# Sums of x's blocks on GpSimd instead of VectorE, and double units three and eight instead of four and seven, in a hybrid decoder trunk

## The chip, the cores and the metric

The kernel runs on one core of one Trainium2 chip: TensorE (PE), VectorE (DVE), ScalarE (ACT), GpSimd (POOL) and SyncE (SP), which work from their own queues, each strictly in the order of its program, and wait for each other on semaphores. The metric is the device time of one execution in microseconds (us).

## The reference

Two layers, each `LN(alpha*x + 0.5*SwiGLU(x))`, `LN(alpha*x + mixer(x))`, `LN(alpha*x + 0.5*SwiGLU(x))`, for 256 positions of width 1024, all in float32. The change touches the SwiGLUs (FFNs), of which there are four:

```python
def swiglu(x, w_in, w_out):
    gate, up = jnp.split(x @ w_in, 2, axis=-1)
    return (jax.nn.silu(gate) * up) @ w_out
```

with `w_in` 1024 x 5632 and `w_out` 2816 x 1024. The mixer (three attention branches, gates, projections) stands between the first and the second FFN of a layer.

## The kernel before

**Tiles.** The 256 positions are two halves, t=0 and t=1, of 128. A float32 product is made of three passes: x and each weight are split into a high and a low part (hi, lo), and TensorE adds x_hi*w_hi, x_hi*w_lo and x_lo*w_hi in one PSUM bank (L585, L586, L587; in double units L784, L786, L787). XH and XL hold the parts of the transposed x of each half, in eight blocks of 128.

**Weights.** A chunk is 128 x 1024 elements, loaded by SyncE into one of seven raw buffers (L306). ScalarE writes its high part (L340) and VectorE, with two SBUF inputs, its low part (L348) into r buffers, of which there are 28. A chunk feeds six matmuls of 512 columns for each half (a turn).

**Units of an FFN.** The 2816 inner columns are eleven units of 256, numbered 0 to 10. `in_unit(u)` makes a unit's gate and up columns (four chunks), `h_chain` its SiLU and product (ScalarE L628, VectorE L630) and its transposed split (ScalarE L488, VectorE L490, which reads a PSUM bank and one SBUF tile). `out_unit` (o0 to o10, two chunks each) multiplies by `w_out`. A **double unit** D covers two units u and u+1 for both halves at once, by seven products P1 to P7 instead of eight (a scheme like Strassen's): joint chunks that serve t=0 and t=1 together, two to a product, 14 in all. Its weights are sums too: VectorE adds chunks (L328), and GpSimd issues DMAs that add into the wide buffers (L318, behind a VectorE addition). Its x operands a2, s2, s4, s3 are sums of x's blocks over both halves, made once in an FFN by `s_chain`: ten additions of 128 x 512 (L654, called through `tt`), and behind each result a split: ScalarE copies the high part (L663), VectorE subtracts (L665). Its results are combined by VectorE (L718, L720, L729).

**Order.** The order of the units in each FFN is the string `FFN` (L64): a number is an `in_unit`, oN an `out_unit`, DN a double unit. A planner in the kernel keeps a clock for each engine (`clk`, `spend`, `V` and `A` for the costs of a VectorE and a ScalarE instruction) and writes each engine's program from it: t=1 follows t=0 by up to seven chunks, and by two around double units. `s_chain` is a generator that starts when x's last block is ready (`hooks`); each `yield` is the time at which it goes on. At the kernel's start VectorE also makes tables for the mixer from about 52 us on (L361 to L438).

Of the kernel before, what the change touches and what calls it, by code (L numbers as in the profile page):

```python
# [57 lines left out]
SEM = 0.4  # L58
# [2 lines left out]

FFN = "0 1 o0 2 o1 3 o2 D4 o3 6 o4 o5 D7 o6 9 o7 10 o8 o9 o10"  # L64
NEAR = 2

MIXER = "qi sm ga0 ka ga1 qa va gc0 qc gc1 oa0 qb oa1 gb0 oc0 oc1 gb1 ob0 ob1"
# [110 lines left out]
def kernel(ctx: ExitStack, tc: tile.TileContext, x, positions, w_in, sink_b, w_br_a, w_br_b, w_br_c,  # L178
                      w_out, ffn1_in, ffn1_out, ffn2_in, ffn2_out, ln_g, ln_b, out):
    nc = tc.nc  # L180
    pe, dve, act, pool = nc.tensor, nc.vector, nc.scalar, nc.gpsimd
# [7 lines left out]
    clk = {"act": 0.0, "dve": 0.0, "pool": 0.0, "dma": 0.0}  # L189

    def spend(engine, cost):
        clk[engine] = max(clk[engine], vt[0]) + cost
        return clk[engine]

    def V(n):
        return spend("dve", 0.07 + 0.00104 * n)

    def A(n, extra=0.1):
        return spend("act", extra + 0.00084 * n)
# [266 lines left out]
    def mark(key, at):  # L466
        ready[key] = at + SEM
        if key in hooks:
            start(hooks.pop(key)(), 1, at + SEM)
# [151 lines left out]
    def ffn(sub, wi2, wo2):  # L621
# [23 lines left out]
        def block(t, h):  # L645
            return [T[t][:, 4 * h:4 * h + 4, :].rearrange("p k c -> p (k c)").bitcast(F32) for T in (XH, XL)]
# [4 lines left out]
        def s_chain():  # L651

            def tt(out, a, b, op):
                dve.tensor_tensor(out, a, b, op=op)  # L654
                return V(512) + 0.05

            def split(name, f):
                while (r := R.take()) is None:
                    yield vt[0] + LATER
                held[0] -= 1  # L660
                yield clk["dve"] + SEM
                hi, lo = r.t[:, :512], r.t[:, 512:]
                act.activation(hi, f.t, AF.Copy)  # L663
                yield A(512) + SEM
                dve.tensor_tensor(lo, f.t, hi.bitcast(F32), op=OP.subtract)  # L665
                mark(("s", sub, name), V(512))
                S[name] = r

            held[0] += 4
            f = []  # L670
            while len(f) < 3:
                if (b := F.take(3)) is None:
                    yield vt[0] + LATER
                else:
                    f.append(b)
            a, b, c = f
            (h11, l11), (h12, l12), (h21, l21), (h22, l22) = (block(*e) for e in ((0, 0), (0, 1), (1, 0), (1, 1)))
            yield tt(a.t, h21, h22, OP.subtract)
            yield tt(b.t, l21, l22, OP.subtract)
            yield tt(a.t, a.t, b.t, OP.add)  # L680
            yield from split("a2", a)
            yield tt(b.t, a.t, h11, OP.subtract)
            yield tt(b.t, b.t, l11, OP.subtract)
            yield from split("s2", b)
            yield tt(c.t, b.t, h12, OP.add)
            yield tt(c.t, c.t, l12, OP.add)
            yield from split("s4", c)
            yield tt(a.t, h11, h21, OP.subtract)
            yield tt(b.t, l11, l21, OP.subtract)
            yield tt(a.t, a.t, b.t, OP.add)  # L690
            yield from split("s3", a)
            for e in f:
                e.free(clk["dve"])
# [160 lines left out]

        steps = FFN.split()
        doubles = [e for e in steps if e[0] == "D"]
# [639 lines left out]
```

## Time and profile before

| | |
|---|---|
| time, median of 3 runs | 1230.28 us (1229.1 to 1230.42) |
| profiled execution, its own time | 1229.19 us |
| its span, first to last instruction | 1227.4 us |
| ScalarE busy | 697.3 us |
| L348, VectorE, low halves of weights | 526.4 us in 440 instructions |
| L340, ScalarE, high halves | 449.1 us in 440 instructions |
| DMA, mean rate | 188 GB/s |

Busy times are sums over the span; the profile's slices are fortieths of the span (30.7 us), each digit a tenth of it. In lists of instructions the columns are the start in us from the span's start, the duration, engine, line, operation, output<-inputs and, in brackets, the idle time before it and what ended that; "x3" merges three that follow each other. In lists of waits the columns are the waiting engine and what it makes, the engine and result waited for, and then us in total, times, longest.

### The profile page before, as it was taken

The numbers are of one execution on the slowest core, as the hardware profiler recorded it, in microseconds if no ns is written. First come the engines' busy times: TensorE is split into PE (matmuls) and PEld (weight loads), VectorE is DVE, ScalarE is ACT, GpSimd is POOL, SyncE is SP. The second block draws the span as 40 slices with busy tenths as digits, with TensorE's granted clock in tenths as the row PEclk, the third lists the DMA queues.
The fourth block names the chain that finished last, engine by engine and source line by source line (L and its number), as shares of the span: only waits on it lengthen the run. The fifth ranks groups of instructions, "written<-read, shape, count | busy, mean of one in ns | idle before, by whom it ended". The sixth has DMA issues, their size and how long they took to land.

```text
span 1227.4 us, 16445 instructions
## 1 busy us (share of the span) xinstructions
PE 1213.3 (99%) x5801; PEld 1007.1 (82%) x5801; DVE 1028.8 (84%) x1677; ACT 697.3 (57%) x1061; POOL 50.5 (4%) x94
## 2 busy tenths in 40 slices
PE   8999999999999999999999999999999999999997
PEld 6888888888887888888888888888888878888886
DVE  7789969996999977888697888699969999788874
ACT  7464744566676545656454755554666665456640
POOL 0101000000000000010000010000000000000100
PEclk9999999999999999999999999999999999999999
DMA  9849685554535755688565678655535467567650
GB/s 339 244 125 286 218 237 158 152 146 145 172 114 178 224 172 177 194 247 269 179 214 159 217 214 291 157 162 155 155 120 154 121 199 235 166 172 249 197 189 35
DMA packets 160179, 231.32 MB, mean 188 GB/s; under 512 B 18272, under 2 KB 79712, under 8 KB 160096
## 3 DMA queue, kind: packets, MB, share of 16 engines
q1 hardware_dynamic: 153760, 215.59, 55.4%
q0 software_dynamic: 6336, 14.68, 5.6%
q8 instruction: 45, 0.74, 0.2%
q14 instruction: 38, 0.31, 0.1%
HBM read 229.19 MB, written 1.05 MB: 188 GB/s over the span
## 4 chain that ended last, share of the span: by engine, by line
PE 91%; DVE 7%; ACT 1%; issue 1%; DVEq 0%; ACTq 0%
PE bank L586 24%; PE bank L587 23%; PE bank L585 23%; PE bank L476 5%; PE bank L786 4%; PE bank L787 4%; PE bank L784 4%; DVE r L348 2%; PE bank L1024 1%; PE bank L1023 1%; PE bank L1196 1%; PE bank L1129 1%; DVE r L974 0%; DVE iacc L1054 0%; ACT r L340 0%
## 5 line engine op out<-in xcount | busy, mean ns | idle before, releaser
L348 DVE TENSOR_TENSOR r<-raw,r 128x1024 fp32r<-128x1024 f32 (+1 forms) x440 | 526.4, 1217 | 49.8 <-ACT r L340 35.6
L340 ACT ACTIVATE r<-raw 128x1024 fp32r<-128x1024 f32 (+1 forms) x440 | 449.1, 1052 | 78.3 <-PE bank L587 17.6
L585 PE MATMUL bank<-r,xh 128*128 128x512 f32 (+1 forms) x928 | 369.5, 398 | 0.0
L586 PE MATMUL bank<-r,xh 128*128 128x512 f32 (+1 forms) x928 | 361.8, 390 | 1.1 <-DVE r L348 1.1
L587 PE MATMUL bank<-r,xl 128*128 128x512 f32 (+1 forms) x928 | 361.9, 390 | 0.0
L587 PEld LDWEIGHTS bank<-r,xl 128*128 128x128 f32 x928 | 174.2, 188 | 36.7 <-DVE xl L490 0.2
L586 PEld LDWEIGHTS bank<-r,xh 128*128 128x128 f32 x928 | 174.7, 188 | 34.9 <-DVE r L348 2.8
L585 PEld LDWEIGHTS bank<-r,xh 128*128 128x128 f32 x928 | 174.5, 188 | 31.9 <-ACT r L340 0.2
L585 PE MATMUL bank<-r,r 128*128 128x512 f32 x448 | 179.8, 401 | 0.0
L587 PE MATMUL bank<-r,r 128*128 128x512 f32 x448 | 175.1, 391 | 0.0
L586 PE MATMUL bank<-r,r 128*128 128x512 f32 x448 | 174.9, 390 | 0.1
L488 ACT ACTIVATE r<-bank 128x256 fp32r<-128x256 f32 (+1 forms) x104 | 49.7, 482 | 119.5 <-PE bank L476 113.9
L587 PEld LDWEIGHTS bank<-r,r 128*128 128x128 f32 x448 | 84.1, 188 | 18.1
L586 PEld LDWEIGHTS bank<-r,r 128*128 128x128 f32 x448 | 84.3, 188 | 16.3 <-DVE r L348 0.9
L585 PEld LDWEIGHTS bank<-r,r 128*128 128x128 f32 x448 | 84.2, 188 | 15.1
L628 ACT ACTIVATE f<-bank 128x256 f32<-128x256 f32 x54 | 20.7, 382 | 114.2 <-PE bank L587 113.8
L490 DVE TENSOR_TENSOR r<-bank,r 128x256 fp32r<-128x256 f32 (+1 forms) x104 | 55.6, 542 | 29.8 <-ACT r L488 28.8
L476 PE MATMUL bank<-ident,f 128*128 128x128 f32 x388 | 61.6, 273 | 2.3 <-DVE f L1176 2.3
L476 PEld LDWEIGHTS bank<-ident,f 128*128 128x128 f32 x388 | 48.6, 140 | 18.0 <-DVE f L1176 4.3
L786 PE MATMUL bank<-r,r 128*128 128x512 f32 x128 | 49.9, 390 | 0.3 <-DVE r L348 0.3
L488 ACT ACTIVATE xh<-bank 128x512 fp32r<-128x512 f32 x32 | 19.1, 597 | 54.4 <-PE bank L476 50.0
L784 PE MATMUL bank<-r,r 128*128 128x512 f32 x128 | 49.9, 390 | 0.0
(193 smaller groups left out, 1290.3 us busy)
## 6 DMA issues: line engine op xcount, KB each, us to landing
raw<-in_ffn_in_dram SPq DMA_DIRECT2D x224, 256.0 KB, 4.0
raw<-in_w_in_dram SPq DMA_DIRECT2D x96, 512.0 KB, 3.7
raw<-in_ffn_out_dram SPq DMA_DIRECT2D x88, 512.0 KB, 4.8
raw<-in_ffn_in_dram SPq DMA_DIRECT2D x48, 512.0 KB, 5.8
wide<-in_ffn_in_dram SPq DMA_DIRECT2D x16, 512.0 KB, 6.2
wide<-in_ffn_in_dram POOLq DMA_DIRECT2D x16, 512.0 KB, 7.2
raw<-in_w_out_dram SPq DMA_DIRECT2D x16, 512.0 KB, 4.7
raw<-in_w_br_a_dram SPq DMA_DIRECT2D x8, 512.0 KB, 3.7
```

Of the source, the lines that this page charges most:

```text
L340: act.activation(pair[0].t[:, :n], source(c), AF.Copy)
L348: dve.tensor_tensor(lo, source(c), h.bitcast(F32), op=OP.subtract)
L476: pe.transpose(bank[:, j * 128:(j + 1) * 128], src[:, j * 128:(j + 1) * 128], ident)
L488: act.activation(hi, v, AF.Copy)
L490: dve.tensor_tensor(lo, v, hi.bitcast(F32), op=OP.subtract)
L585: pe.matmul(o, lhsT=xh(k), rhs=wh, start=k == 0, stop=False)
L586: pe.matmul(o, lhsT=xh(k), rhs=wl, start=False, stop=False)
L587: pe.matmul(o, lhsT=xl(k), rhs=wh, start=False, stop=k == nk - 1)
L628: act.activation(s.t[:, :256], ps.t[:, :256], AF.Silu)
L784: pe.matmul(o, lhsT=hi(k), rhs=wh, start=first and k == 0, stop=False, skip_group_check=not first)
L786: pe.matmul(o, lhsT=hi(k), rhs=wl, start=False, stop=False, skip_group_check=not first)
L787: pe.matmul(o, lhsT=lo(k), rhs=wh, start=False, stop=k == 3, skip_group_check=not first)
```

## The change

The ten sums of `s_chain` are given to GpSimd (`pool.tensor_tensor`), with 1.3 us each in the planner; the splits still run on ScalarE and VectorE, and the planner waits for GpSimd's clock ahead of them and for VectorE's behind them. The string `FFN` has double units three and eight in place of four and seven: unit 2 is now made ahead of o0, and three single units (5, 6, 7) with o2 to o6 stand between the double units where one (6) with o3 to o5 stood.

```diff
@@ -61,7 +61,7 @@
 
 
 
-FFN = "0 1 o0 2 o1 3 o2 D4 o3 6 o4 o5 D7 o6 9 o7 10 o8 o9 o10"
+FFN = "0 1 2 o0 o1 D3 o2 5 o3 6 o4 o5 7 o6 D8 o7 10 o8 o9 o10"
 NEAR = 2
 
 MIXER = "qi sm ga0 ka ga1 qa va gc0 qc gc1 oa0 qb oa1 gb0 oc0 oc1 gb1 ob0 ob1"
@@ -651,20 +651,21 @@
         def s_chain():
 
             def tt(out, a, b, op):
-                dve.tensor_tensor(out, a, b, op=op)
-                return V(512) + 0.05
+                pool.tensor_tensor(out, a, b, op=op)
+                return spend("pool", 1.3) + 0.05
 
             def split(name, f):
                 while (r := R.take()) is None:
                     yield vt[0] + LATER
                 held[0] -= 1
-                yield clk["dve"] + SEM
+                yield clk["pool"] + SEM
                 hi, lo = r.t[:, :512], r.t[:, 512:]
                 act.activation(hi, f.t, AF.Copy)
                 yield A(512) + SEM
                 dve.tensor_tensor(lo, f.t, hi.bitcast(F32), op=OP.subtract)
                 mark(("s", sub, name), V(512))
                 S[name] = r
+                yield clk["dve"]
 
             held[0] += 4
             f = []
```

From L667 on, line numbers of the changed kernel are larger by one.

**VectorE at the start of the first FFN**, before. The raw buffers raw4, raw5, raw6, raw0, raw1, raw2 hold the weight chunks called c4 to c9 in the prediction.

```order
L348 TENSOR_TENSOR r9_101<-raw4_128,r8_100 128x1024
L654 TENSOR_TENSOR f0_91<-xh1_121 128x512
L348 TENSOR_TENSOR r11_103<-raw5_129,r10_102 128x1024
L654 TENSOR_TENSOR f1_133<-xl1_123 128x512
L348 TENSOR_TENSOR r13_105<-raw6_130,r12_104 128x1024
L654 TENSOR_TENSOR f0_91<-f0_91,f1_133 128x512
L630 TENSOR_TENSOR f3_135<-f3_135,bank2_157 128x256
L348 TENSOR_TENSOR r15_107<-raw0_124,r14_106 128x1024
L348 TENSOR_TENSOR r17_109<-raw1_125,r16_108 128x1024
L348 TENSOR_TENSOR r20_112<-raw2_126,r19_111 128x1024
```

The same place with the change:

```order
L348 TENSOR_TENSOR r9_101<-raw4_128,r8_100 128x1024
L348 TENSOR_TENSOR r11_103<-raw5_129,r10_102 128x1024
L348 TENSOR_TENSOR r13_105<-raw6_130,r12_104 128x1024
L630 TENSOR_TENSOR f3_135<-f3_135,bank2_157 128x256
L348 TENSOR_TENSOR r15_107<-raw0_124,r14_106 128x1024
L348 TENSOR_TENSOR r17_109<-raw1_125,r16_108 128x1024
L348 TENSOR_TENSOR r20_112<-raw2_126,r19_111 128x1024
L490 TENSOR_TENSOR r18_110<-bank7_162,r18_110 128x256
L665 TENSOR_TENSOR r21_113<-f0_91,r21_113 128x512
```

The three L654 between the L348 are gone, and L665 (the split of a2) stands two rows behind the L348 of c9. GpSimd's program has the sums at its beginning, behind the four instructions that make constants.

**TensorE at the same place**, before: c5's turn for t=0 (its last three rows), a turn of t=1 (bank5), a pair of transposes, then c6 (r12, r13).

```order
L585 MATMUL bank6_161<-r10_102,xh0_120 128x512
L586 MATMUL bank6_161<-r11_103,xh0_120 128x512
L587 MATMUL bank6_161<-r10_102,xl0_122 128x512
L585 MATMUL bank5_160<-r4_96,xh1_121 128x512
L586 MATMUL bank5_160<-r5_97,xh1_121 128x512
L587 MATMUL bank5_160<-r4_96,xl1_123 128x512
L585 MATMUL bank5_160<-r4_96,xh1_121 128x512
L586 MATMUL bank5_160<-r5_97,xh1_121 128x512
L587 MATMUL bank5_160<-r4_96,xl1_123 128x512
L476 MATMUL bank7_162<-ident_147,f3_135 128x128 x2
L585 MATMUL bank6_161<-r12_104,xh0_120 128x512
L586 MATMUL bank6_161<-r13_105,xh0_120 128x512
```

And with the change:

```order
L585 MATMUL bank6_161<-r10_102,xh0_120 128x512
L586 MATMUL bank6_161<-r11_103,xh0_120 128x512
L587 MATMUL bank6_161<-r10_102,xl0_122 128x512
L476 MATMUL bank7_162<-ident_147,f3_135 128x128 x2
L585 MATMUL bank6_161<-r12_104,xh0_120 128x512
L586 MATMUL bank6_161<-r13_105,xh0_120 128x512
L587 MATMUL bank6_161<-r12_104,xl0_122 128x512
L585 MATMUL bank6_161<-r12_104,xh0_120 128x512
L586 MATMUL bank6_161<-r13_105,xh0_120 128x512
L587 MATMUL bank6_161<-r12_104,xl0_122 128x512
L585 MATMUL bank6_161<-r14_106,xh0_120 128x512
L586 MATMUL bank6_161<-r15_107,xh0_120 128x512
```

The turn of t=1 ahead of c6 is gone; t=0 goes through c6, c7 (r14, r15) and c8 (r16, r17, unit 2) before t=1 has its next turn, and c9 follows that.

**VectorE in the first FFN's first double unit**, before: wide0 and wide1 hold P7's two weight chunks, bank5 the bank of P5 and P3.

```order
L348 TENSOR_TENSOR r0_92<-raw6_130,r11_103 128x1024
L394 TENSOR_SCALAR kk_89<-kk_89 128x64
L328 TENSOR_TENSOR raw2_126<-raw2_126,raw6_130 128x1024
L490 TENSOR_TENSOR r3_95<-bank2_157,r3_95 128x256
L348 TENSOR_TENSOR r13_105<-wide0_144,r1_93 128x1024
L720 TENSOR_TENSOR f4_136<-bank5_160,f4_136 128x512
L348 TENSOR_TENSOR r2_94<-wide1_145,r14_106 128x1024
```

And with the change (bank0 is that bank here, raw2 and raw3 hold P4's chunks):

```order
L369 TENSOR_SCALAR kk_89<-ang_88 128x64
L348 TENSOR_TENSOR r27_119<-wide0_144,r26_118 128x1024
L348 TENSOR_TENSOR r17_109<-wide1_145,r16_108 128x1024
L371 TENSOR_SCALAR kk_89<-kk_89 128x64
L721 TENSOR_TENSOR f11_143<-bank0_155,f11_143 128x512
L348 TENSOR_TENSOR r2_94<-raw2_126,r1_93 128x1024
L381 SCALAR_TENSOR_TENSOR ang_88<-kk_89,ang_88 128x64
L348 TENSOR_TENSOR r23_115<-raw3_127,r22_114 128x1024
L721 TENSOR_TENSOR f10_142<-f10_142,bank4_159 128x512
```

L720 (now L721) stood between P7's two L348; now it stands behind both.

**GpSimd in the second FFN**, with the change; before, this place held only the L545 of the layer norm and then L318.

```order
L654 TENSOR_TENSOR f8_140<-xh1_121 128x512
L654 TENSOR_TENSOR f3_135<-xl1_123 128x512
L654 TENSOR_TENSOR f8_140<-f8_140,f3_135 128x512
L654 TENSOR_TENSOR f3_135<-f8_140,xh0_120 128x512
L654 TENSOR_TENSOR f3_135<-f3_135,xl0_122 128x512
L318 DMA wide0_144<-in_ffn2_in_dram 128x2x512
L654 TENSOR_TENSOR f4_136<-f3_135,xh0_120 128x512
L318 DMA wide1_145<-in_ffn2_in_dram 128x2x512
L654 TENSOR_TENSOR f4_136<-f4_136,xl0_122 128x512
L654 TENSOR_TENSOR f8_140<-xh0_120,xh1_121 128x512
L654 TENSOR_TENSOR f3_135<-xl0_122,xl1_123 128x512
L654 TENSOR_TENSOR f8_140<-f8_140,f3_135 128x512
```

The first three rows make a2, the next two s2, then s4's first sum stands behind one L318 and its second behind another; the last three make s3. The mixers' rows on TensorE stand in the same order in both kernels, but for a few transposes.

## The prediction

> **What bounds the kernel now.** I read the page's busy shares and slices first, then the chain that ended last, then TensorE's own waits, then single stretches.
>
> ```profile
> span 1227.4 us, 16445 instructions
> PE 1213.3 (99%) x5801; PEld 1007.1 (82%) x5801; DVE 1028.8 (84%) x1677; ACT 697.3 (57%) x1061; POOL 50.5 (4%) x94
> ...
> PE   8999999999999999999999999999999999999997
> ...
> DVE  7789969996999977888697888699969999788874
> ...
> PEclk9999999999999999999999999999999999999999
> ...
> PE 91%; DVE 7%; ACT 1%; issue 1%; DVEq 0%; ACTq 0%
> ```
>
> TensorE (PE) is busy in every slice at a full granted clock, and carries 91% of the chain. VectorE (DVE) comes next and touches nine tenths in several slices; GpSimd (POOL) is nearly empty. A busy share can hide pauses, so the next rows are what TensorE waited for after the first 10 us.
>
> ```profile
> PE bank L476 <- DVE f L1176: 2.3, 4, 0.9
> PE bank L586 <- DVE r L348: 0.3, 2, 0.2
> PE bank L786 <- DVE r L348: 0.3, 1, 0.3
> ```
>
> That is 2.9 us in all: 2.3 at the ends of the two mixers, 0.2 of the L586 wait in each mixer, and one 0.3 us wait in the first FFN's first double unit. The change adds and removes no matmul (5801 stay), so **it can win little more than this wait, and can lose whatever VectorE's lateness reaches TensorE.** A measurement of this kernel tells about 0.2% (2.5 us) from no change.
>
> How late VectorE may be is seen where weights go: L348 writes the low half of a weight chunk, L586 (L786 in double units) is its first reader.
>
> ```profile
> 15.79 1.22 DVE L348 TENSOR_TENSOR r<-raw,r 128x1024 fp32r<-128x1024 f32 x1
> 16.92 0.69 DVE L654 TENSOR_TENSOR f<-xh 128x512 f32<-128x512 f32 x1
> 17.53 1.22 DVE L348 TENSOR_TENSOR r<-raw,r 128x1024 fp32r<-128x1024 f32 x1
> 19.27 1.22 DVE L348 TENSOR_TENSOR r<-raw,r 128x1024 fp32r<-128x1024 f32 x1
> 21.34 3.49 DVE L348 TENSOR_TENSOR r<-raw,r 128x1024 fp32r<-128x1024 f32 x3
> ...
> 18.87 0.39 PE L586 MATMUL bank<-r,xh 128*128 128x512 f32 x1
> 19.10 0.39 PE L587 MATMUL bank<-r,xl 128*128 128x512 f32 x1
> 20.23 0.39 PE L586 MATMUL bank<-r,xh 128*128 128x512 f32 x1
> ...
> 23.19 0.40 PE L586 MATMUL bank<-r,xh 128*128 128x512 f32 x1
> 24.56 0.39 PE L586 MATMUL bank<-r,xh 128*128 128x512 f32 x1
> ```
>
> Matmuls of 512 columns start 0.227 us apart (18.87 to 19.10), so a turn of six takes 1.36 us. Call the chunks c4 (written from 15.79), c5 (17.53), c6 (19.27), c7, c8, c9 (the three from 21.34). Their lows end at 17.0, 18.75, 20.5, 22.6, 23.7, 24.8 and TensorE reads c4 to c7 at 18.87, 20.23, 23.19, 24.56. **Early in the first FFN VectorE is only 1.5 to 2.7 us ahead.**
>
> **The change, part by part.** *The sums leave VectorE.* Ten L654 instructions in each of four FFNs (40) go to GpSimd.
>
> ```profile
> L654 DVE TENSOR_TENSOR f<-f,xl x5: 681/685/685, 27.7 to 1065.7; 128x512 f32<-128x512 f32 x5
> ...
> L654 DVE TENSOR_TENSOR wide<-xh x3: 680/680/681, 451.5 to 1056.6; 128x512 f32<-128x512 f32 x3
> ```
>
> They last 0.68 us; between L348s one takes 0.61 (16.92 to 17.53). VectorE is relieved of 40 x 0.61 = 24 us, of which almost nothing lies on TensorE's path, since it waited for an L348 only 0.6 us.
>
> *The same sums on GpSimd* are not in this trace. The nearest rows:
>
> ```profile
> L545 POOL TENSOR_TENSOR rs<-rs,mhalf x12: 545/1456/1542, 183.1 to 1221.6; 128x1 f32<-128x1 f32 x12
> ...
> L406 POOL IOTA f<- 128x256 f32 x1 | 0.8, 832 | 0.0
> ...
> L356 POOL TENSOR_SCALAR_AFFINE_SELECT ident<-ident 128x128 f32<-128x128 f32 x1 | 0.3, 295 | 0.1
> ```
>
> Below: 0.55 us, a TENSOR_TENSOR of one column. Above: IOTA scaled from 256 to 512 columns, 1.66 us. AFFINE_SELECT, which reads and writes, scaled from 128 columns gives 1.18. I take 1.2, the nearest to an instruction that reads SBUF.
>
> [...]
>
> *Do the two engines run beside each other?* L545 does almost no work, yet takes 0.55 to 1.54 us. Two of its executions:
>
> ```profile
> 194.85 1.22 DVE L348 TENSOR_TENSOR r<-raw,r 128x1024 fp32r<-128x1024 f32 x1
> 195.98 0.74 DVE L553 SCALAR_TENSOR_TENSOR y<-y,mv,f 128x512 f32<-128x512 f32 x1
> ...
> 195.02 1.46 POOL L545 TENSOR_TENSOR rs<-rs,mhalf 128x1 f32<-128x1 f32 x1 [10.41 <-DVE rs L543]
> ...
> 444.15 0.41 DVE L490 TENSOR_TENSOR r<-bank,r 128x256 fp32r<-128x256 f32 x1
> ...
> 444.32 0.55 POOL L545 TENSOR_TENSOR rs<-rs,mhalf 128x1 f32<-128x1 f32 x1 [18.67 <-DVE rs L543]
> ```
>
> Begun during an L348 (both inputs in SBUF) it ended at 196.48, 0.41 after that L348 (196.07); begun beside L490 (one input in PSUM) it took 0.55. So GpSimd waits out a running VectorE instruction with two SBUF inputs and is let in before the next. Whether VectorE then waits for a long GpSimd sum no row shows: L545 reads too little. Bounds: nothing, or the sum's whole length each time. I take the whole, since one shared way cannot serve the two at once.
>
> [...]
>
> *The first FFN's start.* Unit 2 now stands before o0, so TensorE reaches the chunks sooner: by the order of its rows c6 is read directly behind c5's turn and one pair of transposes, at about 21.8, c7 at 23.2, c8 at 24.6, and c9 after a t=1 turn at 27.3. Without a shared wait VectorE writes c5 at 18.6, c6 at 19.8, c7 at 22.2, c8 at 23.4 (each 1.13 behind the other, but not before ScalarE's half; L630 keeps its place): still 1.0 us ahead. With strict turns of 1.2 (sum) and 1.22 (L348) the first sum, whose inputs are there by then, runs from 15.28, when the L348 begun at 14.05 ends, and c4 ends at 17.7, c5 20.1, c6 22.55, c7 25.0, c8 27.4, c9 29.8. Lateness: 0.75, 1.8, **2.8**, 2.5. From there on L490 and L630, which have a PSUM input, fill turns and TensorE needs a chunk only every 2.7 us. **Cost: 2.8 us**; 0 if sums take under 0.64 us ((24.6 - 15.28 - 5 x 1.22) / 5); 5.1 at 1.66 (c8 at 29.7).
>
> *The double units move* from four and seven to three and eight; each FFN has the same 14 joint chunks. In the first FFN's double unit the order also changes inside:
>
> ```profile
> 83.44 0.69 DVE L720 TENSOR_TENSOR f<-bank,f 128x512 f32<-128x512 f32 x1 [1.43 <-PE bank L787]
> ...
> 84.05 1.22 DVE L348 TENSOR_TENSOR r<-wide,r 128x1024 fp32r<-128x1024 f32 x1
> ...
> 84.60 0.39 PE L784 MATMUL bank<-r,r 128*128 128x512 f32 x1
> ...
> 85.32 0.50 PE L786 MATMUL bank<-r,r 128*128 128x512 f32 x1 [0.33 <-DVE r L348]
> ```
>
> VectorE waited 1.43 us for a bank at L720 with the second P7 chunk queued behind, and TensorE started its L786 0.72 after its L784 instead of 0.227: 0.5 lost. Now both P7 chunks stand ahead of that combine (L721). **Gain: 0.5 us.** What is late next there is the P4 pair, needed 5.4 us (P7 and P2) after the combine's bank is ready, with 3.1 us of work before it (two L348, one combine, one small one): hidden.
>
> *The second to fourth FFN.* s4's second sum and all of s3's stand on GpSimd behind L318, a DMA that waits for the P5 additions, and behind these sums wait ScalarE's L663 and VectorE's L665. In the second FFN x is ready here:
>
> ```profile
> 448.32 0.60 PE L476 MATMUL bank<-ident,y 128*128 128x128 f32 x4
> ...
> 450.60 0.68 DVE L490 TENSOR_TENSOR xl<-bank,xh 128x512 fp32r<-128x512 f32 x1
> ...
> 440.00:480.00 40.00, 40.00 (x187) 33.03 (x186) 31.72 (x45) 18.02 (x27) 0.55 (x1) 1.00 0.40 123
> ```
>
> By the new order VectorE has from the end of this L490 (451.3) to P7's last low half 21 instructions of 1.13 us (L348, L328), 4 L665 of 0.61 and 9 L490 or L630 of 0.34: 29.2 us. TensorE gets there after 187 matmuls and 10 transposes of 0.11, counted from x's last transpose 2.5 us before: 42.5 + 1.1 - 2.5 = 41.1. Ten sums of 1.2 make VectorE's side 41.2, less the 3.1 us of L490 and L630 that need no turn: 38.1, a cover of 3.0 us. (The third FFN starts with more chunks ready.) VectorE is idle 8.3 of the 40 us in the last row; such gaps take in sums for nothing, or eat the cover if they remain. Cost: nothing. SyncE's loads into wide1 no longer wait for sums in that buffer (the sums take f buffers now). The mixers' rows on TensorE stand as before, so their 2.6 us of waits stay.
>
> Sum against the profiled execution's own 1229.19 us (its span, 1227.42, and 1.8 around it; the runs' median is 1230.28, so it lies 1.1 below within their spread): 1229.2 - 0.5 + 2.8 = **1231.5 us**.
>
> **The rivals.**
> 1. *No shared wait, or a short one.* VectorE is only relieved and 0.5 us is won: 1228.7. For it: no row shows VectorE waiting for GpSimd. Against: L545's ends follow VectorE's. 22%.
> 2. *Slower: GpSimd's sums take turns with L348 and are long.* Place: c6 to c9 of the first FFN, then P7 of the second and fourth. At 1.66 the first FFN loses 5.1; in the second and fourth 29.2 + 16.6 - 3.1 = 42.7 stands against 41.1, 1.6 each: 1229.2 - 0.5 + 5.1 + 3.2 = 1237.0. It decides from about 1.35 us a sum on, where the first FFN alone loses 3.5 (1232.2, over 0.2% more than the profiled execution); so 1232.5 to 1237. For it: IOTA's pace. Against: AFFINE_SELECT's. 25%.
> 3. *The sums don't run beside.* They queue behind L318 so that the work is only later: as hidden as today while the cover of 3.0 us holds; 1229.2 or 1228.7. 4%.
> 4. *Faster by over 0.2%.* It would need most of the 2.9 us of waits, of which 2.6 lie in mixers that do not change. 4%.
>
> **How the numbers follow.** Forecast 45%; rivals 22, 25, 4 and 4%. A fifth of the forecast (sums of 1.3 and over) falls beyond 0.2%: slower 25 + 9 = 34%, faster 4%, the rest, 62%, within. The range goes from 1228.4 (rival 1 with 0.3 of spread) to 1235.5, inside rival 2; about 2 in 10 are left out.
>
> **What would show it.** GpSimd's sums near 1.2 us alone and up to 2.4 behind an L348; single L348s of the first FFN lasting 2.4 or starting 1.2 late between 15 and 30 us; TensorE waits L586 <- L348 of 2 to 3 us in sum between 20 and 28 us; no wait at L787 in the first double unit; the mixers' waits as before. The forecast is wrong if L348 keeps its 1.22 us and 1.13 spacing beside the sums (rival 1), or if TensorE waits around P6, P7 in the later FFNs (rival 2).

## The result, and the profile after

| | before | changed |
|---|---|---|
| time, median of 5 runs each | 1229.16 us (1229.1 to 1230.42) | 1242.65 us (1241.52 to 1244.86) |
| ratio | | 1.0106, 95% interval 1.0091 to 1.0121 |
| profiled execution, its own time | 1229.19 us | 1241.6 us |

The change makes the kernel 1.1% slower. The prediction, 1231.5 us with a range to 1235.5 and most of its chance on no change, is wrong. The page of the changed kernel, the lines that answer to those of before:

```profile
span 1239.5 us, 16465 instructions
...
PE 1215.5 (98%) x5801; PEld 1007.4 (81%) x5801; DVE 1038.2 (84%) x1637; ACT 697.8 (56%) x1061; POOL 115.6 (9%) x134
...
PE   8999999999999999999999999999999999999997
...
DVE  7987889996999979858888858899979999797684
...
PE 84%; DVE 12%; issue 2%; DMA 1%; ACT 1%; SPq 0%; DVEq 0%; ACTq 0%
```

TensorE executes the same 5801 matmuls. VectorE lost 40 instructions (1677 to 1637) and yet became *busier*, 1028.8 to 1038.2 us, and its share of the chain that ended last rose from 7 to 12%. In slices of 31 us TensorE still looks full; its waits, in the list of waits (engine and its result, what it waited for, then us in total, times, longest), tell where the time went:

```profile
PE bank L476 <- DVE f L630: 8.5, 5, 2.1
PE bank L476 <- DVE f L1177: 2.3, 4, 0.9
PE bank L586 <- DVE r L348: 2.1, 5, 0.8
```

The second row is the mixers' old wait, unchanged. The first row is new, 8.5 us in five places: TensorE's transposes (L476) of an `h_chain`'s product (L630). Three of the five are 2.1 us long and lie one each in the second, third and fourth FFN; two (0.91 and 1.25 us) lie in the first. Of the third row 0.59 us, at 26.9 us in the first FFN, is new as well. Here is the second FFN in the list of instructions, VectorE first, then GpSimd, then TensorE:

```profile
474.48 0.41 DVE L490 TENSOR_TENSOR r<-bank,r 128x256 fp32r<-128x256 f32 x1
475.18 7.17 DVE L348 TENSOR_TENSOR r<-raw,r 128x1024 fp32r<-128x1024 f32 x2 [0.29 <-ACT r L340]
482.27 0.68 DVE L665 TENSOR_TENSOR r<-f,r 128x512 fp32r<-128x512 f32 x1
482.88 1.22 DVE L328 TENSOR_TENSOR raw<-raw,raw 128x1024 f32<-128x1024 f32 x1
484.01 1.21 DVE L348 TENSOR_TENSOR r<-raw,r 128x1024 fp32r<-128x1024 f32 x1
485.15 1.21 DVE L328 TENSOR_TENSOR raw<-raw,raw 128x1024 f32<-128x1024 f32 x1
486.28 0.41 DVE L630 TENSOR_TENSOR f<-f,bank 128x256 f32<-128x256 f32 x1
...
475.18 4.94 DVE L348 TENSOR_TENSOR r<-raw,r 128x1024 fp32r<-128x1024 f32 x1 [0.29 <-ACT r L340]
...
473.97 1.22 POOL L318 DMA_DIRECT2D wide<-in_ffn_in_dram  x1 [2.58 <-PE bank L476]
474.77 1.76 POOL L654 TENSOR_TENSOR f<-f,xl 128x512 f32<-128x512 f32 x1
476.03 1.75 POOL L654 TENSOR_TENSOR f<-xh,xh 128x512 f32<-128x512 f32 x1
477.28 1.75 POOL L654 TENSOR_TENSOR f<-xl,xl 128x512 f32<-128x512 f32 x1
479.10 2.17 POOL L654 TENSOR_TENSOR f<-f,f 128x512 f32<-128x512 f32 x1
...
486.75 0.44 PE L476 MATMUL bank<-ident,f 128*128 128x128 f32 x2 [2.13 <-DVE f L630]
```

Two L348, 2.4 us of work, last 7.17 us together (the list merges them in one row; the row behind it has the first alone). The first, 4.94 us long, begins 0.4 us after GpSimd's first sum (L654) and ends after the third; the second is held by the fourth. L630, which reads PSUM and is not held itself, stands five instructions behind in VectorE's queue, and TensorE waits 2.13 us for it.

### The profile page after: what moved, and what is told of

Same layout as the page of the kernel before. It is cut to its first block, busy times and chain, and to the rows that moved or that the text cites. A ratio compares the mean times of both kernels' runs of the same rounds, so it can differ in the third digit from the quotient of the medians.

```text
span 1239.5 us, 16465 instructions
## 1 busy us (share of the span) xinstructions
PE 1215.5 (98%) x5801; PEld 1007.4 (81%) x5801; DVE 1038.2 (84%) x1637; ACT 697.8 (56%) x1061; POOL 115.6 (9%) x134
## 4 chain that ended last, share of the span: by engine, by line
PE 84%; DVE 12%; issue 2%; DMA 1%; ACT 1%; SPq 0%; DVEq 0%; ACTq 0%
PE bank L586 22%; PE bank L587 22%; PE bank L585 22%; DVE r L348 5%; PE bank L476 4%; PE bank L788 4%; PE bank L787 4%; PE bank L785 4%; PE bank L1025 1%; PE bank L1024 1%; PE bank L1130 1%; PE bank L1197 1%; DVE raw L328 0%; DMA raw<-in_ffn_in_dram 0%; ACT r L340 0%
## 5 line engine op out<-in xcount | busy, mean ns | idle before, releaser
L348 DVE TENSOR_TENSOR r<-raw,r 128x1024 fp32r<-128x1024 f32 (+1 forms) x440 | 549.4, 1271 | 45.1 <-ACT r L340 32.4
L586 PE MATMUL bank<-r,xh 128*128 128x512 f32 (+1 forms) x928 | 361.9, 390 | 2.1 <-DVE r L348 2.1
L587 PE MATMUL bank<-r,xl 128*128 128x512 f32 (+1 forms) x928 | 362.0, 390 | 0.0
L587 PEld LDWEIGHTS bank<-r,xl 128*128 128x128 f32 x928 | 174.2, 188 | 36.8
L586 PEld LDWEIGHTS bank<-r,xh 128*128 128x128 f32 x928 | 174.8, 188 | 35.6 <-DVE r L348 4.2
L585 PE MATMUL bank<-r,r 128*128 128x512 f32 x448 | 179.0, 400 | 0.0
L586 PE MATMUL bank<-r,r 128*128 128x512 f32 x448 | 175.5, 392 | 0.2
L587 PE MATMUL bank<-r,r 128*128 128x512 f32 x448 | 175.5, 392 | 0.0
L587 PEld LDWEIGHTS bank<-r,r 128*128 128x128 f32 x448 | 84.5, 189 | 18.1
L586 PEld LDWEIGHTS bank<-r,r 128*128 128x128 f32 x448 | 84.7, 189 | 17.1 <-DVE r L348 1.0
L490 DVE TENSOR_TENSOR r<-bank,r 128x256 fp32r<-128x256 f32 (+1 forms) x104 | 55.6, 541 | 39.4 <-ACT r L488 38.9
L476 PE MATMUL bank<-ident,f 128*128 128x128 f32 x400 | 64.1, 274 | 10.7 <-DVE f L630 8.5
L476 PEld LDWEIGHTS bank<-ident,f 128*128 128x128 f32 x400 | 49.8, 140 | 28.3 <-DVE f L630 10.6
L630 DVE TENSOR_TENSOR f<-f,bank 128x256 f32<-128x256 f32 x56 | 23.2, 415 | 34.3 <-ACT f L628 34.2
L785 PE MATMUL bank<-r,r 128*128 128x512 f32 x128 | 50.2, 392 | 0.0
L318 POOL DMA_DIRECT2D wide<-in_ffn_in_dram x16 | 19.7, 1230 | 323.8 <-DVE raw L328 309.7
```

The costliest lines, as they stand in the source:

```text
L348: dve.tensor_tensor(lo, source(c), h.bitcast(F32), op=OP.subtract)
L476: pe.transpose(bank[:, j * 128:(j + 1) * 128], src[:, j * 128:(j + 1) * 128], ident)
L490: dve.tensor_tensor(lo, v, hi.bitcast(F32), op=OP.subtract)
L585: pe.matmul(o, lhsT=xh(k), rhs=wh, start=k == 0, stop=False)
L586: pe.matmul(o, lhsT=xh(k), rhs=wl, start=False, stop=False)
L587: pe.matmul(o, lhsT=xl(k), rhs=wh, start=False, stop=k == nk - 1)
```

## The experiments

Three theories. **Hold**: a GpSimd sum keeps VectorE's two-input instructions out while it reads SBUF, and what stands behind them comes late. **Order**: the new string `FFN` alone puts the transposes too close behind their product. **Queue**: the sums stand in GpSimd's queue behind L318 and come late to their own readers (L663, L665).

### One half of the change at a time

The new order with the sums on VectorE:

```diff
 (before)
-FFN = "0 1 o0 2 o1 3 o2 D4 o3 6 o4 o5 D7 o6 9 o7 10 o8 o9 o10"
+FFN = "0 1 2 o0 o1 D3 o2 5 o3 6 o4 o5 7 o6 D8 o7 10 o8 o9 o10"
```

> The new string FFN, with the ten sums of each FFN back on VectorE. Theory H (hold): a GpSimd sum keeps VectorE's instructions with two SBUF inputs out while it runs, and sums that do not depend on each other, standing in a row, keep them out for all of them; VectorE's products (L630) queue behind the held L348, and TensorE's transposes of them (L476) wait. By H nothing is lost here: 1228.0 to 1229.7 us, no wait of L476 for L630, no L348 above 1.25 us. Theory O (order): the new order puts the transposes so close behind the product they need that TensorE waits for it whoever makes the sums: about 1238 to 1242 us, with waits L476 <- L630 of about 2 us in FFNs two to four. Theory Q (queue): the sums come late because they stand in GpSimd's queue behind the adding DMAs (L318), and their readers wait: like H here, 1228 to 1229.7.

Measured: 1229.59 us against 1229.84 of before beside it, ratio 0.9999 (0.999 to 1.0008); no wait of L476 for L630. The string is no cause, and brings nothing that can be measured either. (From the same string the planner writes somewhat other programs when VectorE makes the sums; the kernel without reads, below, has the changed kernel's own rows.) Its opposite, the old order with the sums on GpSimd:

> The old string FFN (double units four and seven) with the sums on GpSimd. Theory H: still slower, since the same ten sums hold VectorE out, but by what stands behind the held instructions in the old order; estimate 1233 to 1242 us, with L348 of 3.5 us or more wherever three independent sums run in a row. Theory O: 1229 to 1231, since the order is the old one. Theory Q: in the old order all ten sums of an FFN stand ahead of the adding DMAs, so nothing makes them late: 1228.5 to 1231.

Measured: 1236.45 us, ratio 1.0053 (1.004 to 1.0065). Slower, so the sums are the cause here too; by another set of places (the longest new wait is 1.56 us at L587 for L490 in the first FFN; TensorE's listed waits grow from 6.2 to 9.6 us in all, which places about half of the 6.6 us), and no L348 above 2.32 us, which the theory of hold had wrong: three independent sums in a row did not suffice to make the 5 us. In this order all sums of an FFN stand ahead of its adding DMAs, so queue cannot be it.

### The sums without their reads

```diff
 (changed)
-                pool.tensor_tensor(out, a, b, op=op)
+                pool.memset(out, 0.5)
```

> The changed kernel with each of the ten sums an FFN replaced by a GpSimd write of a constant into the same 128x512 buffer (the sums are left out): the same rows on every other engine, the same place in GpSimd's queue and the same waits, but no SBUF input on GpSimd. Theory H, with the hold coming from GpSimd's reads: L348 stays at 1.25 us or less, L476 does not wait for L630, 1228 to 1230 us. If the hold comes from GpSimd's writes too, it stays slower in proportion to the write's length. Theory O and theory Q: 1238 to 1243 us, since order and queue are as in the changed kernel.

Measured: 1229.32 us, ratio 0.9998 (0.9989 to 1.0007), with VectorE's, ScalarE's and TensorE's rows all as in the changed kernel. The groups by line in the changed kernel (busy us, mean ns):

```profile
L348 DVE TENSOR_TENSOR r<-raw,r 128x1024 fp32r<-128x1024 f32 (+1 forms) x440 | 549.4, 1271 | 45.1 <-ACT r L340 32.4 <-PE bank L587 5.4 <-issue 3.3
L328 DVE TENSOR_TENSOR raw<-raw,wide 128x1024 f32<-128x1024 f32 x16 | 22.2, 1387 | 0.3
L665 DVE TENSOR_TENSOR r<-f,r 128x512 fp32r<-128x512 f32 x16 | 17.6, 1098 | 0.3
```

And in the kernel without reads:

```profile
L654 POOL MEMSET f<- 128x512 f32 x40 | 23.2, 710 | 27.6 <-DVE r L665 23.3 <-PE bank L1411 4.1
L348 DVE TENSOR_TENSOR r<-raw,r 128x1024 fp32r<-128x1024 f32 (+1 forms) x440 | 526.2, 1218 | 48.5 <-ACT r L340 35.7 <-PE bank L587 5.4 <-issue 3.2
L328 DVE TENSOR_TENSOR raw<-raw,wide 128x1024 f32<-128x1024 f32 x16 | 19.6, 1222 | 0.3
L665 DVE TENSOR_TENSOR r<-f,r 128x512 fp32r<-128x512 f32 x16 | 11.0, 688 | 0.8 <-ACT r L663 0.4
```

23.2 + 2.6 + 6.6 = 32.4 us of VectorE's time are hold, more than the 24 that the change took off it. The list of instructions also gives the slack of the product in the second FFN, undisturbed:

```profile
478.13 0.42 DVE L630 TENSOR_TENSOR f<-f,bank 128x256 f32<-128x256 f32 x1
...
481.14 0.27 PE L476 MATMUL bank<-ident,f 128*128 128x128 f32 x1
```

L630 ends at 478.55, TensorE comes for it at 481.14: **2.6 us early**. In the changed kernel L630 ends at 486.69 and TensorE had come at 484.62 (486.75 - 2.13), so it was 2.6 + 2.1 = 4.7 us late against the undisturbed kernel: four sums of 1.17. One write is also shorter than a sum (0.71 us on average in the list above); the control has three writes for each sum (1.6 us):

> The changed kernel with each sum replaced by three writes of a constant in a row (the sums are left out), so that GpSimd is as long busy as with the sums, 3 x 0.52 = 1.6 us for each, still without an SBUF input. Rows, order and waits of all other engines as in the changed kernel. Theory H: 1228.5 to 1230.5 us as with one write, no wait of L476 for L630. If what the single write removed was GpSimd's time (0.7 us in place of 1.3 to 2.2) and not its reads: 1236 to 1242.

Measured: 1229.4 us, ratio 1.0 (0.9991 to 1.0009), no wait for L630. It is the reading, not GpSimd's time or queue.

### One sum after the other

If totals decide, TensorE loses only what exceeds the 2.6 us. First the three sums of s3 as writes, which leaves one real sum (the last of s4) ahead of L630:

```diff
 (changed; a last argument False makes a write of a constant)
-            yield tt(a.t, h11, h21, OP.subtract)
-            yield tt(b.t, l11, l21, OP.subtract)
-            yield tt(a.t, a.t, b.t, OP.add)
+            yield tt(a.t, h11, h21, OP.subtract, False)
+            yield tt(b.t, l11, l21, OP.subtract, False)
+            yield tt(a.t, a.t, b.t, OP.add, False)
```

> The changed kernel, with the three sums of s3 in each FFN replaced by writes of a constant (s3 is left out; the seven others are made as in the change). Other engines have the same rows. Theory H, by totals: in FFNs two and four the product L630 that TensorE waits for is 2.6 us early without sums (in the run with no reads it ends at 478.55 and its transposes start at 481.14) and the last sum of s4 with the three of s3 make it 4.7 late. With the three gone it is at most 1.2 to 2.4 late, so the waits L476 <- L630 of 2.1 us there vanish, in the third FFN as well, and the time falls by 6.2 to 8 us to 1234.5 to 1236.5. If the loss came from the late reading of the sums (ScalarE L663 and VectorE L665) it would stay at 1241.5 to 1243.5.

Then with only the last two, and only the last of them, as writes:

> As the last, with the second and third of s3's sums as writes; one sum of s3 and the last of s4 stand ahead of L630. Theory H by totals: 2 x 1.2 = 2.4 us late against 2.6, so no wait over 0.3 us at L476 in FFNs two and four; 1232.3 to 1233.8 us, as with all three as writes, although an L348 of about 3.7 us stays. If every hold cost in proportion: 1232.8 + (1242.6 - 1232.8) / 3 = 1236.

> The changed kernel with the last of s3's three sums in each FFN replaced by a write of a constant (s3 is wrong by that; the other nine sums are made). Ahead of the product L630 in FFNs two to four stand then three holds instead of four. Theory H by totals: 3 x 1.2 = 3.6 us late against 2.6 of slack, so waits L476 <- L630 of about 1.0 us in each of FFNs two to four; 1232.8 (with s3's sums all as writes) + 3 x 1.0 = 1235.8 us, 1235.0 to 1237.0. If the loss belonged to the row of three independent sums, which still stands (an L348 of 4.9 us): nothing changes, 1241.5 to 1243.5.

The second FFN's L476 with two and with three sums ahead of L630, in the list of instructions of the two kernels. Two:

```profile
483.63 0.41 DVE L630 TENSOR_TENSOR f<-f,bank 128x256 f32<-128x256 f32 x1
...
484.17 0.39 PE L476 MATMUL bank<-ident,f 128*128 128x128 f32 x2
```

Three:

```profile
485.67 0.33 PE L476 MATMUL bank<-ident,f 128*128 128x128 f32 x1 [1.03 <-DVE f L630]
```

| sums ahead of L630 | longest L348, second FFN | L476 waits, second FFN | time, median | ratio |
|---|---|---|---|---|
| 0 (no reads at all) | 1.2 us | 0 | 1229.32 | 0.9998 (0.9989 to 1.0007) |
| 1 (s3 as writes) | 2.46 | 0 | 1232.79 | 1.0023 (1.0013 to 1.0032) |
| 2 | 3.68 | 0 | 1233.68 | 1.0029 (1.0018 to 1.0041) |
| 3 | 4.94 | 1.03 | 1237.64 | 1.0066 (1.0052 to 1.008) |
| 4 (changed) | 4.94, then the next held too | 2.13 | 1242.65 | 1.0106 (1.0091 to 1.0121) |

Each row has its own runs of before beside it (medians 1229.16 to 1230.21 us), and the ratio is against these. With two sums L630 ends at 484.04 and TensorE comes at 484.17: the slack is used to the last tenth, and every further sum costs 1.0 to 1.1 us there. The time with three sums missed its range by 0.6: I had put the third FFN's slack equal to the others', and it is smaller. There L630 stands directly behind the held L348; TensorE waits 0.84 us for it with two sums and 2.06 with three already, and the fourth holds only the L665 behind it. The time with one sum came out 1.7 below its range, so s3's sums cost 9.9 us in all and not only the 6.3 of these three waits. Row against row with the kernel without reads, each wait costs 0.2 us more than its listed length, which makes 7.0, and in the profiled execution a slower clock behind one of them adds 1.4 (last section); where the other 1.5 us lie was not found. The wait of 0.91 us in the first FFN is gone too with s3 as writes, but it doesn't hang on s3's sums: it ends at 22.8 us, and the first of them starts at 30.89. TensorE's clock was 0.66 from 9 to 14 us in that execution (1.00 in the changed kernel's), so that it came to the product 0.8 us later.

### Does it matter that three ran in a row?

The changed kernel with the sums of s3 each made upon the one before:

```diff
 (changed)
             yield tt(a.t, h11, h21, OP.subtract)
-            yield tt(b.t, l11, l21, OP.subtract)
-            yield tt(a.t, a.t, b.t, OP.add)
+            yield tt(a.t, a.t, l11, OP.add)
+            yield tt(a.t, a.t, l21, OP.subtract)
```

> The changed kernel with the three additions of s3 made one upon the other (a = h11-h21, a = a+l11, a = a-l21) instead of two independent ones and their sum; VectorE, ScalarE and TensorE have the same rows. Theory H with starvation by a row of independent sums: the row of three (the last of s4, the first two of s3) becomes a row of two, so the longest L348 falls from 5.0 us to about 3.8, each wait L476 <- L630 of FFNs two to four falls from 2.1 to about 0.9 us, and the time to 1237.5 to 1239.5 us. If instead turns are strict and the 5 us have another cause (say, the length of the GpSimd instruction itself): unchanged, 1241.5 to 1243.5, with an L348 of 5 us. Theory O and theory Q: unchanged, 1241.5 to 1243.5.

Measured: 1240.88 us (1239.64 to 1242.32), ratio 1.009 (1.0076 to 1.0104). The longest L348 of the second FFN fell to 3.68 us as expected, but the time missed its range, since the wait there fell only to 1.96: the third sum now holds the L665 ahead of L630 instead. Only in the third FFN did it fall, to 0.82, and the first FFN has a new one of 0.59. A row makes one instruction very late; what reaches TensorE is the sum of the holds ahead of the product, however they are dealt out.

### The first FFN alone

The ten sums of the first FFN as writes, the others as in the change:

> The changed kernel, with all ten sums of the first FFN replaced by writes of a constant (they are left out), the other three FFNs as in the change. Theory H: TensorE's waits in the first FFN behind 20 us go (L476 <- L630 at 22.8 and 32.3 and L586 <- L348 at 26.9, 1.1 + 1.4 + 0.75 = 3.2 us of pitch lost), so 1239.0 to 1240.0 us, and 2.1 us each stays in FFNs two to four. If the first FFN's loss were of the order or of the start: 1242 to 1243.

Measured: 1238.88 us, ratio 1.0076 (1.0063 to 1.0088). So the first FFN's sums cost 3.8 us, and all the rest of the loss is behind it; TensorE's wait for L630 is 6.3 us in three places, 2.1 each, as expected (the time lies 0.1 us below its range).

### Can the planner be told?

```diff
 (changed)
                 pool.tensor_tensor(out, a, b, op=op)
-                return spend("pool", 1.3) + 0.05
+                spend("dve", 1.2)
+                return spend("pool", 2.5) + 0.05
```

> The changed kernel with the planner told what a sum costs: 2.5 us on GpSimd in place of 1.3, and 1.2 us of VectorE's clock for each sum; the order on all engines follows from it. The sums still hold VectorE. Theory H: the hold itself stays (L348 mean near 1.26 us, VectorE's total as in the change), but products and weight chunks are placed ahead of it, so most of TensorE's waits go: 1231 to 1237 us. If the holds fall elsewhere than planned, since planner and chip disagree on when sums run: 1238 to 1243. Under 1229, faster than before, is expected by neither.

Measured: 1239.71 us, ratio 1.0082 (1.0069 to 1.0096), in the second of the two ranges: the holds fall elsewhere than planned. TensorE hardly waits for L630 any more (0.2 us) but 4.2 us for low halves of the double units (L788 here, L786 of the kernel before), a wait that the change did not have. The other try gave out s3's sums later:

```diff
 (changed)
             yield from split("s4", c)
+            yield clk["dve"] + 6.0
             yield tt(a.t, h11, h21, OP.subtract)
```

> The changed kernel with the three sums of s3 given out by the planner 6 us later, all sums made. Theory H: only the last sum of s4 then stands ahead of the product L630 that TensorE waits for, so the waits L476 <- L630 in FFNs two to four fall under 0.5 us, as with those sums as writes; the three holds of about 1.1 us fall on weight chunks of the double unit instead. If VectorE is ahead enough there: 1232 to 1235 us; if it isn't (as with both engines charged, where TensorE waited 4.2 us at L788 for L348): 1236 to 1241.

Measured: 1244.26 us, ratio 1.0125 (1.0112 to 1.0139). The edit did not do what it was for: in the second to fourth FFN GpSimd's sums kept their place behind the same L318 (an L348 of 4.92 us again, waits of 2.1), since a planner's delay is no wait on the chip, and the later L665 made TensorE wait 2.1 us more.

### The hold by itself

A kernel of its own puts twelve VectorE subtractions of 128x1024 beside a few GpSimd instructions:

> A kernel of its own, which computes nothing of the trunk: twelve VectorE subtractions of 128x1024 with both inputs in SBUF (the form of L348), beside them on GpSimd in turn: three independent sums of 128x512; three sums each on the one before; six independent; six each on the one before; six copies (one SBUF input); five writes of a constant; then six independent sums beside VectorE instructions that have one input in PSUM, and six with VectorE idle. Theory H with starvation: the first VectorE instruction that meets a row of n independent sums waits for all of them, about 3.7 + 1.2 us for three and 7.5 + 1.2 for six; with dependent sums each waits for one, 2.3 us, three or six times; copies hold too; writes and PSUM inputs do not (1.22 and 0.7 us throughout), and a sum alone takes 1.29 us. Theory of strict turns: 2.3 us at most in all the rows of sums. Either way VectorE loses about 1.1 to 1.25 us a sum in all.

Its list of instructions (VectorE's twelve merged in one row each): three independent sums, three chained, six independent, six chained, six copies, five writes; then sixteen VectorE instructions with a PSUM input beside six sums, and six sums alone.

```profile
5.38 16.91 DVE L213 TENSOR_TENSOR o<-xa,xb 128x1024 f32<-128x1024 f32 x12 [0.46 <-DMA xb<-in_x_dram]
...
23.54 16.90 DVE L213 TENSOR_TENSOR o<-xa,xb 128x1024 f32<-128x1024 f32 x12
...
41.69 20.10 DVE L213 TENSOR_TENSOR o<-xa,xb 128x1024 f32<-128x1024 f32 x12
...
63.03 20.10 DVE L213 TENSOR_TENSOR o<-xa,xb 128x1024 f32<-128x1024 f32 x12
...
84.37 16.18 DVE L213 TENSOR_TENSOR o<-xa,xb 128x1024 f32<-128x1024 f32 x12
...
101.79 13.71 DVE L213 TENSOR_TENSOR o<-xa,xb 128x1024 f32<-128x1024 f32 x12
...
116.75 9.65 DVE L217 TENSOR_TENSOR o<-xa,bank 128x512 f32<-128x512 f32 x16
...
127.80 7.35 POOL L275 TENSOR_TENSOR s<-g,xb 128x512 f32<-128x512 f32 x6 [3.49 <-DVE g L206]
```

Beside writes the twelve take 13.71 us, with three sums 3.2 more, with six 6.4 more: **1.07 us of VectorE for each sum**, dependent or not. Copies cost 0.41 each. Instructions with a PSUM input keep their 0.6 us. A sum alone takes 7.35 / 6 = 1.2 us. Here independent sums took strict turns (2.28 us for each held subtraction), against the theory of a row. The second kernel tried other beginnings of a row:

> A kernel of its own, which computes nothing of the trunk: rows of four independent sums on GpSimd beside twelve VectorE subtractions of 128x1024: first behind a sum that waits for VectorE; then behind a DMA that GpSimd issues, as in FFNs two to four; then started by ScalarE while VectorE has no instruction with two SBUF inputs, whose subtractions begin in the middle of the first sum; and the same with four sums each on the one before. In the first kernel of this kind independent sums took turns like dependent ones (2.28 us each), unlike the 4.94 us L348. If what lets a row of sums through is that GpSimd had the port before VectorE asked: the third stretch shows one VectorE instruction of 4.5 us or more, the fourth none above 2.4. If it is the DMA ahead: the second shows it and the third not. If neither, all stay at 2.3.

No subtraction of it exceeded 2.32 us, behind a plain DMA of 128x512 neither. In its third stretch VectorE came just as the first sum ended, so the case that it was made for did not arise. The third kernel put the adding DMA ahead, as in the trunk:

> A kernel of its own, which computes nothing of the trunk: rows of four sums on GpSimd behind the adding DMA of 128x2x512 of the form of L318, independent, then each on the one before, beside VectorE subtractions of 128x1024; then independent behind that DMA and behind none, with four VectorE instructions with a PSUM input first, so that its first subtraction comes in the middle of the row. If a GpSimd row that has the port keeps it: the last two stretches show a subtraction of 3.5 us or more. If it needs the adding DMA: the first and third do, the last doesn't. If neither: 2.3 us in all, and the 4.9 us of the changed kernel stay unexplained.

Its list of instructions: the long subtraction of the first stretch, the twelve of the first and the second stretch, and the long one of the third.

```profile
7.60 6.72 DVE L213 TENSOR_TENSOR o<-xa,xb 128x1024 f32<-128x1024 f32 x1
...
6.46 19.20 DVE L213 TENSOR_TENSOR o<-xa,xb 128x1024 f32<-128x1024 f32 x12
...
28.05 18.53 DVE L213 TENSOR_TENSOR o<-xa,xb 128x1024 f32<-128x1024 f32 x12
...
51.35 5.22 DVE L213 TENSOR_TENSOR o<-xa,xb 128x1024 f32<-128x1024 f32 x1
```

Behind an adding DMA of 128x2x512 four independent sums run through (6.72 and 5.22 us for one subtraction); chained ones take turns (2.85 us at most), and in the fourth stretch, without that DMA, so do independent ones that are under way when VectorE comes (2.28 at most). So in these stretches it took both, that DMA ahead and sums that do not depend on each other. That DMA is also the larger of the two that were tried (128x2x512 against the plain one of 128x512); whether its adding or its size does it, and why, stays open.

## Why the prediction was wrong

- *TensorE bounds, 2.9 us to win, mixers unchanged:* right. The mixers' 2.3 us stand; the wait in the first double unit is gone, but 0.5 us in 1230 is less than can be told (the order alone: 0.9999).
- *A sum takes 1.2 us on GpSimd:* right, 1.2 alone and 2.2 behind a VectorE instruction.
- *The two engines take turns:* right. The kernel of the hold alone shows three things: VectorE instructions with two SBUF inputs lose 1.07 us to each sum that GpSimd makes beside them, they lose nothing to its writes (13.71 us for the twelve, 1.13 from start to start), and instructions with one input in PSUM lose nothing to its sums (9.65 us for sixteen, 0.6 each). That one shared way cannot serve the two engines at once was my assumption, and so was "the port" of two expectations; the runs show the turns, not what makes them. My first rival, no shared wait, falls.
- *VectorE is relieved of 24 us:* wrong once turns are assumed, and the prediction did not draw that line: 24 us saved against 32.4 us of hold. Over the whole kernel that is still idle time of VectorE; where it is not, it decides.
- *First FFN, 2.8 us at L586 for L348:* the size of the waits was right, 2.75 us in the profiled execution (0.91, 0.59 and 1.25), but only 0.59 of it at the named place; the rest is at L476 for L630. By medians the first FFN costs 3.8, a term 1 us too small.
- **The step that failed is "The second to fourth FFN ... Cost: nothing".** It measured VectorE's lateness at one deadline, P7's last low half, at the end of a stretch of 41 us, and found a cover of 3.0 us. A nearer deadline lies inside that stretch: the product L630, 2.6 us early, with four sums in the 12 us ahead of it, which come together behind L318 (in the third FFN three sums, with less slack). The working even took L490 and L630 off the bill as instructions "that need no turn". They need none (0.6 us each beside six sums, as above), but stand in VectorE's queue behind instructions that do. Measured: 2.13, 2.06 and 2.12 us of waits in place of nothing.
- *Rival 2, slower:* the right side, by a condition that did not come true (sums of 1.35 us and longer), and at places (P6, P7) where nothing waited.

The account of the profiled execution, 12.4 us: waits for L630 in FFNs two to four 6.3, new waits in the first FFN 2.75, about 1.4 of slower clock behind the wait in the third FFN (below). Each of the six waits costs 0.22 to 0.29 us more than its listed length, row against row with the kernel without reads, 1.4 in all. Some 0.5 us is left, of the size by which starts of single runs differ (TensorE's waits for x at L476 are 0.3 to 2.3 us in all in the profiled executions). By medians the account is that of the experiments: 1242.65 with all sums, 1238.88 without the first FFN's, 1232.79 without s3's, 1229.32 with none.

## What to carry to other kernels

Giving GpSimd work that reads SBUF did not take it off VectorE, whose instructions beside it have both inputs in SBUF: here a sum cost VectorE 0.61 us to make, and 1.07 to be held for wherever VectorE was busy (32.4 us for 40 sums, 0.81 on average). Whoever estimates such a move asks, for every instruction in the held engine's queue and not only for the held kind, when its reader comes, and counts how many holds fall between; a mean cover over a long stretch hides the one product that is 2.6 us early. Neither half of this change was worth having: the sums on GpSimd cost time in either order, and with them on VectorE the new order is as fast as the old one.

## What was not expected of the hardware

A row of independent GpSimd sums behind an adding DMA kept VectorE out for all of them (4.94 to 6.72 us for one subtraction), where otherwise the two engines took turns (2.28 us for a held subtraction). And behind a pause TensorE lost, in some executions, more than the pause itself. The windows of the changed kernel (from and to, length, TensorE's busy time, its granted clock, DMA share, GB/s) behind the wait of 2.06 us in the third FFN:

```profile
654.00:657.00 3.00, 3.00 (x14) 1.00 0.77 91
659.20:661.20 2.00, 2.00 (x8) 0.75 0.00 0
661.20:664.00 2.80, 2.80 (x8) 0.57 0.00 0
```

The clock falls from 1.00 to 0.57 and seven matmuls start 0.2 us further apart (0.43 us in place of the 0.227 before the wait), 1.4 us in all. Behind equal waits in the second and fourth FFN (2.13 and 2.12 us) it does not fall (1.00 from 486.8 to 492 us and from 1098.2 to 1104 us), and in the kernel with three sums, behind a wait of 2.06 us at the same place, it stays at 1.00. Without the first FFN's sums it falls there as well (0.50 from 658.1 to 660 us), and with both engines charged it falls behind two shorter waits, of 0.94 us (ending at 65.48) and 0.76 us (at 66.74):

```profile
68.00:72.00 4.00, 4.00 (x12) 0.60 0.36 109
```

The five runs of the changed kernel took 1241.5 and 1241.6 us at a mean granted clock of 0.998, and 1242.7 to 1244.9 at 0.992 to 0.995; that more such falls made the latter longer is likely, but not shown. So behind a pause of 2.06 us the clock fell in one profiled execution and not in another, and once it fell behind two pauses under 1 us. What decides it was not tried.
